# S5 mixer: a batch's output and gelu emitted one iteration later, its tables one iteration nearer; transposes tied to a matmul in the second FFN's input

## The chip, the cores and the metric

One core of one Trainium2 chip. The metric is the device time of one execution in microseconds (us). Engines: PE (TensorE, matmuls and transposes), DVE (VectorE), ACT (ScalarE), POOL (GpSimd), SP (issues DMAs).

## The reference

A decoder trunk of two layers over 512 positions of 1024 channels, float32. Layer 0 mixes by a diagonal complex state-space layer (S5), layer 1 by differential attention; each is followed by a gated convolutional FFN and a gated per-layer projection. The change lies mainly in the S5 mixer, which is:

```python
u = h @ w_in
bu_r = jnp.einsum("tbgc,gpc->tbgp", u_chunk, bb_r)
bu_i = jnp.einsum("tbgc,gpc->tbgp", u_chunk, bb_i)
pw_r, pw_i, s_r, s_i = lax.associative_scan(_ssm_combine, (a_r, a_i, bu_r, bu_i), axis=0)
x_r = s_r + pw_r * x_r0 - pw_i * x_i0
x_i = s_i + pw_r * x_i0 + pw_i * x_r0
y = einsum("tbgp,gcp->tbgc", x_r, cr) - einsum("tbgp,gcp->tbgc", x_i, ci)
...
y = y + d_skip * u
g = jax.nn.gelu(y)
val, gate = jnp.split(g @ w_glu, 2, axis=-1)
return val * jax.nn.sigmoid(gate)
```

There are 64 groups of 16 channels with 64 complex states each.

## The kernel before

All matrix products with weights are made as three float32r matmuls of a high and a low part (`mm3`, L121 to L125); ACT casts a weight tile to its high part (`hi_wst`, L107, L112), DVE makes the low part (`lo_wst`, L108, L113). A program-wide scheduler orders the instructions of each engine by the order in which they are emitted, moving one ahead of others where its operands are ready; so the order of the Python statements gives priorities, and the order that came out is shown below.

**The mixer** (`ssm`, L629 to L713) handles the 64 groups as 8 batches of 8. For batch b these steps are made, by the names that the rows carry:

- `ssm_coefs` and `cprod` (L491 to L498, DVE): the products `wo` of C and the powers. `wo` has one buffer.
- `ssm_prep` (L511 to L528): ACT spreads `wo` into zero-padded operands, `wp` (for the inputs) and `op` (for the outputs; both L504, `pad`); PE transposes `wp` (`ct`, L526, two banks), ACT copies it to `ctrl` (L527). `op` has two buffers, `wp` one.
- `ssm_tables` (L454 to L479): rotation tables `tab` of sines and cosines, DVE at L464 and L467, ACT at L466 (`rnd`) and L474 to L478 (Sin and Abs); POOL spreads the decay (L471).
- `ssm_turn_u` (L557, L559): PE transposes the batch's inputs (`ut`), ACT copies them to `uc`.
- `ssm_toep` (L530 to L550): the short-range block, PE at L536 and L546 into the bank `toep`, ACT copies at L547 and L549.
- `ssm_inputs` (L568): `v`, 16 matmuls into two banks. `ssm_states` (DVE L587, L588, L589, L591 twice, L592, L593, L596): rotate, scan, rotate back, into `xs`.
- `ssm_out` (PE L605, L609, ACT L612): `y`, then gelu into `g`. Gelu and Sin need different tables of ACT, so an ACT_TABLE_LOAD stands before the first of either kind.
- `ssm_turn` (PE L621, ACT L625, DVE L626): `g` transposed (`gt`) and split into `hTh` and `hTl` for the next product.

Steps of neighbouring batches are interleaved in one loop, b from -2 to 9. Between them PE works on two weight products in steps: the second half of `w_in` (`u1`), and the first quarter of `w_glu` (`gv`), step k of which needs `hTh`, `hTl` of batch k. The banks `ct` (both), `ut`, `toep`, `gt` and `y` all rotate over the same two PSUM banks (tag "tp"); a bank is free for the next when its reader, an ACT copy or the gelu, is done.

**The second place** is the input projection of the second FFN behind the attention (L923 to L931): `flush_turns` emits the transposes of a normed row block between the matmul steps of `project_k` (L811).

Of the kernel before, what the change touches and what calls it, by code (L numbers as in the profile page):

```python
# [10 lines left out]
F32 = mybir.dt.float32  # L11
# [7 lines left out]
P = 128  # L19
# [3 lines left out]
KD = D // P  # L23
# [33 lines left out]
class Trunk:  # L57
# [62 lines left out]
    def mm3(self, out, lhs, rhs, start, stop):  # L120
        nc = self.nc  # L121
        (ah, al), (bh, bl) = lhs, rhs
        nc.tensor.matmul(out, ah, bh, start=start, stop=False)  # L123
        nc.tensor.matmul(out, ah, bl, start=False, stop=False)  # L124
        nc.tensor.matmul(out, al, bh, start=False, stop=stop)  # L125

    def norm(self, nm):

# [382 lines left out]
    def ssm_prep(self, sp, b, coefs):  # L511

        nc = self.nc
        bc, wo = coefs
        wp = sp.tile([P, 8, 4, 2, 16], F32, tag="wp", name=f"wp{b}", bufs=1)
        self.pad(wp, wo[:, :, 0])
        op = sp.tile([P, 8, 5, 2, 16], F32, tag="op", name=f"op{b}", bufs=2)
        self.pad(op[:, :, 1:], wo[:, :, 1])
        self.pad(op[:, :, 0:1], bc[:, :, 1].rearrange("p r q (o c) -> p r q o c", o=1))
        op = op.rearrange("p (r q) n g c -> p r q (n g c)", r=2)  # L520
        wp = wp.rearrange("p (r q) n g c -> p r q (n g c)", r=2)
        ctrl = sp.tile([P, 2, 512], F32, tag="ctrl", name=f"ctrl{b}", bufs=2)
        for r in range(2):
            ps = self.bank(f"ct{b}_{r}", "tp")
            for q in range(4):
                nc.tensor.transpose(ps[:, q * P:(q + 1) * P], wp[:, r, q, :], self.ident)  # L526
            nc.scalar.copy(ctrl[:, r, :], ps)  # L527
        return ctrl, wp, op  # L528

    def ssm_toep(self, sp, b, wp, op):  # L530
# [97 lines left out]
    def ssm(self, nxt):  # L628
        nc, tc, io = self.nc, self.tc, self.io  # L629
        with ExitStack() as ctx:  # L630
            sp = ctx.enter_context(tc.tile_pool(name="ssm", bufs=1))
            st = self.ssm_load(sp)


            n, copied = Raw(self, "ssm"), []
            u0 = Accumulate(self, io["w_in"][0], "u0")
            for c in range(2):
                for j in range(4):
                    self.turn(self.x[j], j, c, "ssm", ("tp", "aux")[j % 2])
                    if c == 0:  # L640
                        copied.append(self.copied)
                for k in range(4):
                    if k % 2 == 0:
                        i = 2 * c + k // 2
                        u0.w.append(self.split(st[i], self.gssm[:, 2 * i:2 * i + 2]))
                    u0.step(4 * c + k)
                if c == 0:
                    self.ssm_params(sp)
            for j in range(4):
                with tc.issue_after(copied[j].ins):  # L650
                    n.scale(j)
            U = self.xall.rearrange("p a b -> p (a b)")
            Uv = U.rearrange("p (q j e) -> p q j e", j=4, e=32)

            def done(nb):
                def f(j, ps):
                    nc.scalar.activation(Uv[:, nb * 16:(nb + 1) * 16, 3 - j, :], ps.rearrange("p (q e) -> p q e", e=32),
                                         AF.Copy, scale=n.rs[:, j:j + 1])
                return f

            for j in range(4):
                done(0)(j, u0.ps[j])
            gv = Accumulate(self, io["w_glu"][0], "gv0")
            u1 = Accumulate(self, io["w_in"][1], "u1", g=self.gssm)

            tab, coefs, prep, toep, uc, ins, xs, gs = ({} for _ in range(8))
            on = lambda n: 0 <= n < 8
            for b in range(-2, 10):
                if on(b + 1):
                    prep[b + 1] = self.ssm_prep(sp, b + 1, coefs[b + 1])  # L670
                if on(b):
                    xs[b] = self.ssm_states(sp, b, ins[b], tab[b])
                if on(b + 1):
                    uc[b + 1] = self.ssm_turn_u(sp, b + 1, U)
                    toep[b + 1] = self.ssm_toep(sp, b + 1, *prep[b + 1][1:])
                for k in GV.get(b, ()):
                    gv.step(k)
                if on(b - 1):
                    self.ssm_turn(b - 1, gs[b - 1])
                if on(b + 1):  # L680
                    ins[b + 1] = self.ssm_inputs(b + 1, uc[b + 1], prep[b + 1][0])
                if on(b):
                    gs[b] = self.ssm_out(sp, b, prep[b][2], toep[b], uc[b], xs[b])
                if on(b + 2):
                    tab[b + 2] = self.ssm_tables(sp, b + 2)
                for k in U1.get(b, ()):
                    u1.step(k)
                    if k == KD - 1:
                        for j in range(4):
                            done(1)(j, u1.ps[j])  # L690
                if on(b + 2):
                    coefs[b + 2] = self.ssm_coefs(sp, b + 2)
            self.load_x()
            self.load_conv(0)
            for nb in range(2):
                val = {}

                def keep(t, ps):
                    if t % 2 == 0:
                        val[t // 2] = sp.tile([P, 2, 512], F32, tag="ctrl", name=f"val{nb}_{t}", bufs=2)  # L700
                    nc.scalar.copy(val[t // 2][:, t % 2], ps)

                def gate(t, ps):
                    s = sp.tile([P, 512], F32, tag="g", name=f"gate{nb}_{t}", bufs=2)
                    nc.scalar.activation(s, ps, AF.Sigmoid)
                    nc.vector.tensor_tensor(s, s, val[t // 2][:, t % 2], ALU.mult)
                    self.add_x(t, nb, s)

                if nb == 0:
                    for t in range(NT):  # L710
                        keep(t, gv.ps[t])
                else:
                    self.project(io["w_glu"][nb], f"gv{nb}", False, keep)  # L713
                self.project(io["w_glu"][nb + 2], f"gg{nb}", True, gate, nxt=nxt if nb else None, split=KD // 2 - 2 * nb,
                             behind=None if nb else self.rotated)
# [94 lines left out]

    def project_k(self, ps, w, t, k0, k1, c=slice(0, 512)):  # L811
        for k in range(k0, k1):
            self.mm3(ps[:, c], self.hT(k, t), [z[:, c] for z in self.rhs(w, k)], k == 0, k == KD - 1)

    def head_norm(self, ps, nb, t, dst, ap, nm, scale, ident, me):

# [25 lines left out]
    def attention(self, me, nxt):  # L842


        nc, tc, io = self.nc, self.tc, self.io
        with ExitStack() as ctx:
# [6 lines left out]
            c = (qT, kT, v, strip, sg, ap)  # L853
# [23 lines left out]
            for b in (keys, queries, values):  # L877
                f = b(0)
# [18 lines left out]
            wo = []  # L897
# [12 lines left out]
            n = nxt()  # L910
            w = self.weights(io["w_o"][1])
            ps = [self.bank(f"wo1_{t}") for t in range(NT)]
# [5 lines left out]
            for t in back:  # L918
                if t == 1:
                    po = self.bank("wo0_0", "aux")  # L920
                    self.project_k(po, wo, 0, 0, 4)
                    n(2)
                    self.flush_turns()  # L923
                    self.project_k(po, wo, 0, 4, KD)
                    self.add_x(0, 0, po)
                self.project_k(ps[t], w, t, 4, 6)
                if t == 1:
                    self.flush_turns()
                self.project_k(ps[t], w, t, 6, KD)
                if t in (2, 0):  # L930
                    n(t + 1)  # L931
                self.add_x(t, 1, ps[t])
# [239 lines left out]
```

## Time and profile before

| | us |
|---|---|
| median of 3 runs (1340.53 to 1341.23) | 1340.82 |
| the profiled execution | 1340.96 |
| its span in the trace | 1339.2 |
| PE busy | 1316.7 (98%) |
| DVE busy | 780.6 (58%) |
| ACT busy | 615.8 (46%) |

The profile is one execution; busy shares are means over the whole span, and the mixer, which is the first eighth of it, looks different from the rest. So the rows further down are those of the mixer's batches.

### The profile page before, as it was taken

To read this page: it belongs to the slowest core of one execution; us is meant where nothing else is said; L and a number is where in the kernel's file an instruction comes from. 1 tells how busy PE (TensorE), PEld (TensorE's weight loads), DVE (VectorE), ACT (ScalarE), POOL (GpSimd) and SP (SyncE) were. 2 spreads that over 40 slices of the span, in tenths; PEclk is the share of its full clock that TensorE was granted. 3 is DMA by queue.
4 is the path that set the end of the run, shared out by engine and by line. 5 is a ranking of instruction groups with operands and counts; after the bars stand their busy time and mean duration, and the time that the engine had idled before them with its cause. 6 is when DMAs were issued, how large, how long until landed. Compare 5 with 4: busy or idle time off the path is not lost.

```text
span 1339.2 us, 16754 instructions
## 1 busy us (share of the span) xinstructions
PE 1316.7 (98%) x6524; PEld 1084.4 (81%) x6524; DVE 780.6 (58%) x1305; ACT 615.8 (46%) x1049; POOL 90.3 (7%) x101
## 2 busy tenths in 40 slices
PE   7999899999999999999999999999999999999998
PEld 5887788987888888888887776689888888888887
DVE  8999734666633566443544665746766435664343
ACT  7899524444421444243545565635444313443241
POOL 2153000000000000000030121000000000000000
PEclk9999999999999999999999999999999999999999
DMA  6311322333333333322423102113333333333311
GB/s 220 106 41 52 111 95 79 101 94 98 92 110 94 96 99 102 100 80 94 138 85 126 63 1 86 42 47 111 111 95 95 109 95 96 98 105 95 95 56 40
DMA packets 37099, 122.31 MB, mean 91 GB/s; under 512 B 4339, under 2 KB 6387, under 8 KB 37020
## 3 DMA queue, kind: packets, MB, share of 16 engines
q1 hardware_dynamic: 35804, 119.07, 28.3%
q10 hardware_dynamic: 1184, 2.16, 0.5%
q8 instruction: 51, 0.84, 0.3%
q14 instruction: 28, 0.23, 0.1%
q0 software_dynamic: 32, 0.02, 0.0%
HBM read 119.12 MB, written 2.12 MB: 91 GB/s over the span
## 4 chain that ended last, share of the span: by engine, by line
PE 87%; DVE 9%; ACT 2%; issue 1%; DMA 0%; POOL 0%; SPq 0%; ACTq 0%; DVEq 0%
PE up L123 12%; PE up L124 12%; PE up L125 12%; PE dn L123 6%; PE dn L124 6%; PE dn L125 6%; PE pg L125 2%; PE pg L124 2%; PE pg L123 2%; PE s L982 2%; PE o L1004 1%; DVE zb L591 1%; PE k L123 1%; PE q L123 1%; PE gg L125 1%; PE gg L124 1%
## 5 line engine op out<-in xcount | busy, mean ns | idle before, releaser
L108 DVE TENSOR_TENSOR lo_wst<-wst,hi_wst 128x1024 fp32r<-128x1024 f32 x162 | 197.6, 1223 | 258.2 <-ACT hi_wst L107 257.9
L123 PE MATMUL up<-hTh,hi_wst 128*128 128x512 f32 (+1 forms) x768 | 285.6, 372 | 0.0
L124 PE MATMUL up<-hTl,hi_wst 128*128 128x512 f32 (+1 forms) x768 | 285.2, 371 | 0.0
L125 PE MATMUL up<-hTh,lo_wst 128*128 128x512 f32 (+1 forms) x768 | 285.2, 371 | 0.0
L107 ACT CAST hi_wst<-wst 128x1024 fp32r<-128x1024 f32 x162 | 169.6, 1049 | 227.7 <-PE dn L125 143.1
L123 PEld LDWEIGHTS up<-hTh,hi_wst 128*128 128x128 f32 x768 | 144.7, 188 | 25.3 <-ACT hi_wst L107 0.2
L125 PEld LDWEIGHTS up<-hTh,lo_wst 128*128 128x128 f32 x768 | 144.7, 188 | 24.9
L124 PEld LDWEIGHTS up<-hTl,hi_wst 128*128 128x128 f32 x768 | 144.7, 188 | 24.7
L123 PE MATMUL dn<-hi_wst,ih 128*128 128x512 f32 x352 | 137.6, 391 | 0.0
L124 PE MATMUL dn<-lo_wst,ih 128*128 128x512 f32 x352 | 137.0, 389 | 0.0
L125 PE MATMUL dn<-hi_wst,il 128*128 128x512 f32 x352 | 136.4, 389 | 0.0
L247 DVE SCALAR_TENSOR_TENSOR acc<-up,cw,acc 128x511 f32<-128x511 f32 x88 | 65.7, 747 | 47.8 <-ACT acc L246 47.8
L246 ACT ACTIVATE acc<-up,cw 128x512 f32<-128x512 f32 x88 | 68.5, 779 | 47.8 <-PE up L125 47.8
L254 ACT CAST ih<-acc 128x512 fp32r<-128x512 f32 x44 | 27.3, 620 | 112.9 <-DVE acc L251 112.8
L123 PEld LDWEIGHTS dn<-hi_wst,ih 128*128 128x128 f32 x352 | 66.1, 188 | 14.6 <-issue 1.0
L113 DVE SCALAR_TENSOR_TENSOR lo_wst<-wst,gains,hi_wst 128x512 fp32r<-128x512 f32 x80 | 56.1, 745 | 37.0 <-ACT hi_wst L112 37.0
L125 PEld LDWEIGHTS dn<-hi_wst,il 128*128 128x128 f32 x352 | 66.1, 188 | 13.7
L124 PEld LDWEIGHTS dn<-lo_wst,ih 128*128 128x128 f32 x352 | 66.1, 188 | 13.4
L248 DVE SCALAR_TENSOR_TENSOR acc<-up,cw,acc 128x510 f32<-128x510 f32 x88 | 65.8, 748 | 2.9
L112 ACT ACTIVATE hi_wst<-wst,gains 128x512 fp32r<-128x512 f32 x80 | 53.4, 718 | 28.0 <-PE dn L125 16.9
L250 ACT ACTIVATE acc<-acc 128x512 f32<-128x512 f32 x44 | 27.8, 632 | 64.9 <-DVE acc L248 64.8
L125 PE MATMUL pg<-hi_wst,hTl 128*128 128x512 f32 (+1 forms) x128 | 49.2, 384 | 0.0
(271 smaller groups left out, 2215.1 us busy)
## 6 DMA issues: line engine op xcount, KB each, us to landing
wst<-in_w_up SPq DMA_DIRECT2D x88, 512.0 KB, 3.6
wst<-in_w_down SPq DMA_DIRECT2D x44, 512.0 KB, 3.6
wst<-in_w_glu SPq DMA_DIRECT2D x16, 512.0 KB, 4.0
wst<-in_w_gate SPq DMA_DIRECT2D x16, 512.0 KB, 3.5
wst<-in_kv_w SPq DMA_DIRECT2D x16, 512.0 KB, 4.5
wst<-in_w_in SPq DMA_DIRECT2D x8, 512.0 KB, 6.8
wst<-in_w_q SPq DMA_DIRECT2D x8, 512.0 KB, 3.8
wst<-in_w_o SPq DMA_DIRECT2D x8, 512.0 KB, 4.4
```

The source lines that it names most:

```text
L107: nc.scalar.copy(hi, st)
L108: nc.vector.tensor_tensor(lo, st, hi.bitcast(F32), ALU.subtract)
L112: nc.scalar.activation(hi[:, c], st[:, c], AF.Copy, scale=g[:, k:k + 1])
L113: nc.vector.scalar_tensor_tensor(lo[:, c], st[:, c], g[:, k:k + 1], hi[:, c].bitcast(F32), ALU.mult, ALU.subtract)
L123: nc.tensor.matmul(out, ah, bh, start=start, stop=False)
L124: nc.tensor.matmul(out, ah, bl, start=False, stop=False)
L125: nc.tensor.matmul(out, al, bh, start=False, stop=stop)
L246: nc.scalar.activation(c, ps[s], AF.Identity, bias=self.cw[:, n, 3:4], scale=self.cw[:, n, 2:3])
L247: nc.vector.scalar_tensor_tensor(c[:, 1:], ps[s][:, :T - 1], self.cw[:, n, 1:2], c[:, 1:], ALU.mult, ALU.add)
L248: nc.vector.scalar_tensor_tensor(c[:, 2:], ps[s][:, :T - 2], self.cw[:, n, 0:1], c[:, 2:], ALU.mult, ALU.add)
L250: nc.scalar.activation(acc[0], acc[0], AF.Gelu_apprx_tanh)
L254: nc.scalar.copy(ih, acc[1])
```

## The change

Three edits:

1. In `ssm_prep` the four pads of `op` are emitted behind the transposes and the copies of `ctrl`.
2. In the loop, `ssm_tables(b+1)` stands right behind `ssm_prep(b+1)`, where before `ssm_tables(b+2)` stood near the end of iteration b; and `ssm_out` of batch b-1 stands in iteration b, behind the prep and the tables of batch b+1 and ahead of `ssm_states(b)`, where before `ssm_out(b)` stood in iteration b behind `ssm_inputs(b+1)`.
3. `project_k` returns its last matmul, and in the second FFN's input `flush_turns` at t = 1 is emitted under `tc.issue_after` of it.

```diff
--- before.py
+++ after.py
@@ -122,7 +122,7 @@
         (ah, al), (bh, bl) = lhs, rhs
         nc.tensor.matmul(out, ah, bh, start=start, stop=False)
         nc.tensor.matmul(out, ah, bl, start=False, stop=False)
-        nc.tensor.matmul(out, al, bh, start=False, stop=stop)
+        return nc.tensor.matmul(out, al, bh, start=False, stop=stop)
 
     def norm(self, nm):
 
@@ -514,10 +514,6 @@
         bc, wo = coefs
         wp = sp.tile([P, 8, 4, 2, 16], F32, tag="wp", name=f"wp{b}", bufs=1)
         self.pad(wp, wo[:, :, 0])
-        op = sp.tile([P, 8, 5, 2, 16], F32, tag="op", name=f"op{b}", bufs=2)
-        self.pad(op[:, :, 1:], wo[:, :, 1])
-        self.pad(op[:, :, 0:1], bc[:, :, 1].rearrange("p r q (o c) -> p r q o c", o=1))
-        op = op.rearrange("p (r q) n g c -> p r q (n g c)", r=2)
         wp = wp.rearrange("p (r q) n g c -> p r q (n g c)", r=2)
         ctrl = sp.tile([P, 2, 512], F32, tag="ctrl", name=f"ctrl{b}", bufs=2)
         for r in range(2):
@@ -525,6 +521,10 @@
             for q in range(4):
                 nc.tensor.transpose(ps[:, q * P:(q + 1) * P], wp[:, r, q, :], self.ident)
             nc.scalar.copy(ctrl[:, r, :], ps)
+        op = sp.tile([P, 8, 5, 2, 16], F32, tag="op", name=f"op{b}", bufs=2)
+        self.pad(op[:, :, 1:], wo[:, :, 1])
+        self.pad(op[:, :, 0:1], bc[:, :, 1].rearrange("p r q (o c) -> p r q o c", o=1))
+        op = op.rearrange("p (r q) n g c -> p r q (n g c)", r=2)
         return ctrl, wp, op
 
     def ssm_toep(self, sp, b, wp, op):
@@ -668,6 +668,9 @@
             for b in range(-2, 10):
                 if on(b + 1):
                     prep[b + 1] = self.ssm_prep(sp, b + 1, coefs[b + 1])
+                    tab[b + 1] = self.ssm_tables(sp, b + 1)
+                if on(b - 1):
+                    gs[b - 1] = self.ssm_out(sp, b - 1, prep[b - 1][2], toep[b - 1], uc[b - 1], xs[b - 1])
                 if on(b):
                     xs[b] = self.ssm_states(sp, b, ins[b], tab[b])
                 if on(b + 1):
@@ -679,10 +682,6 @@
                     self.ssm_turn(b - 1, gs[b - 1])
                 if on(b + 1):
                     ins[b + 1] = self.ssm_inputs(b + 1, uc[b + 1], prep[b + 1][0])
-                if on(b):
-                    gs[b] = self.ssm_out(sp, b, prep[b][2], toep[b], uc[b], xs[b])
-                if on(b + 2):
-                    tab[b + 2] = self.ssm_tables(sp, b + 2)
                 for k in U1.get(b, ()):
                     u1.step(k)
                     if k == KD - 1:
@@ -810,7 +809,8 @@
 
     def project_k(self, ps, w, t, k0, k1, c=slice(0, 512)):
         for k in range(k0, k1):
-            self.mm3(ps[:, c], self.hT(k, t), [z[:, c] for z in self.rhs(w, k)], k == 0, k == KD - 1)
+            mm = self.mm3(ps[:, c], self.hT(k, t), [z[:, c] for z in self.rhs(w, k)], k == 0, k == KD - 1)
+        return mm
 
     def head_norm(self, ps, nb, t, dst, ap, nm, scale, ident, me):
 
@@ -923,9 +923,10 @@
                     self.flush_turns()
                     self.project_k(po, wo, 0, 4, KD)
                     self.add_x(0, 0, po)
-                self.project_k(ps[t], w, t, 4, 6)
+                mm = self.project_k(ps[t], w, t, 4, 6)
                 if t == 1:
-                    self.flush_turns()
+                    with tc.issue_after(mm.ins):
+                        self.flush_turns()
                 self.project_k(ps[t], w, t, 6, KD)
                 if t in (2, 0):
                     n(t + 1)
```

Below, the order that came out, for the last batches. A name's first number is the batch (`ct7_1` is the second `ct` bank of batch 7), the rest tells buffers apart; `gv0_2` and its like are the weight product.

PE, the output `y5` before the change:

```order
L605 MATMUL y5_1384<-toep1_296,uc5_1197 128x128 x4
L609 MATMUL y5_1384<-op5_1160,xs5_1311 128x128 x8
L123 MATMUL gv0_0_1077<-hi_wst10_1543_1545,hTh_82 128x512
L124 MATMUL gv0_0_1077<-lo_wst10_1543_1546,hTh_82 128x512
L526 MATMUL ct7_0_1434<-ident_67,wp7_1425 128x128 x4
```

and further on in the same order, up to the first inputs `v7_0`:

```order
L526 MATMUL ct7_1_1440<-ident_67,wp7_1425 128x128 x4
L125 MATMUL gv0_2_1079<-hi_wst10_1543_1545,hTl_83 128x512
L123 MATMUL gv0_3_1080<-hi_wst10_1543_1545,hTh_82 128x512
L124 MATMUL gv0_3_1080<-lo_wst10_1543_1546,hTh_82 128x512
L125 MATMUL gv0_3_1080<-hi_wst10_1543_1545,hTl_83 128x512
L557 MATMUL ut7_1460<-ident_67,x_81 128x128 x4
L536 MATMUL toep7_1467<-op7_1428,wp7_1425 32x128 x8
L546 MATMUL toep7_1467<-dm7_1476,ident_67 32x32 x4
L621 MATMUL gt5_1498<-ident_67,g5_1397 128x128 x4
L568 MATMUL v7_0_1505<-uc7_1465,ctrl7_1433 128x128 x4
```

PE after the change, up to the same `v7_0`:

```order
L522 MATMUL ct7_0_1400<-ident_67,wp7_1396 128x128 x4
L522 MATMUL ct7_1_1406<-ident_67,wp7_1396 128x128 x4
L124 MATMUL gv0_3_1080<-lo_wst10_1543_1546,hTh_82 128x512
L125 MATMUL gv0_3_1080<-hi_wst10_1543_1545,hTl_83 128x512
L605 MATMUL y5_1431<-toep1_296,uc5_1197 128x128 x4
L609 MATMUL y5_1431<-op5_1144,xs5_1311 128x128 x8
L557 MATMUL ut7_1460<-ident_67,x_81 128x128 x4
L536 MATMUL toep7_1467<-op7_1412,wp7_1396 32x128 x8
L546 MATMUL toep7_1467<-dm7_1476,ident_67 32x32 x4
L621 MATMUL gt5_1498<-ident_67,g5_1444 128x128 x4
L568 MATMUL v7_0_1505<-uc7_1465,ctrl7_1399 128x128 x4
```

`y5` stood ahead of both `ct7`; now it stands behind both, directly ahead of `ut7` and `toep7`.

ACT before the change, from the second half of the pad `wp7` to the high part of `gt5`:

```order
L504 ACTIVATE wp7_1425<-wo7_1415,s5_87 128x32x16
L612 ACT_TABLE_LOAD
L612 ACTIVATE g5_1397<-y5_1384 128x4x4x32
L504 ACTIVATE op7_1428<-wo7_1415,s5_87 128x8x4x16 x2
L504 ACTIVATE op7_1428<-bc7_1413,s5_87 128x8x16 x2
L527 COPY ctrl7_1433<-ct7_0_1434 128x512
L527 COPY ctrl7_1433<-ct7_1_1440 128x512
L559 COPY uc7_1465<-ut7_1460 128x512
L547 COPY toep1_296<-toep7_1467 32x512
L625 CAST hTh_82<-gt5_1498 128x512
```

ACT after it, from the first copy of `ctrl7` (`wp7` and three rows of `tab7` stand just above):

```order
L523 COPY ctrl7_1399<-ct7_0_1400 128x512
L523 COPY ctrl7_1399<-ct7_1_1406 128x512
L476 ACTIVATE rnd7_1419<-ang7_1417 128x256
L477 ACTIVATE tab7_1422<-rnd7_1419,halfpi_201 128x4x64
L478 ACTIVATE tab7_1422<-rnd7_1419,halfpi_201 128x4x64
L504 ACTIVATE op7_1412<-wo7_1386,s5_87 128x8x4x16 x2
L504 ACTIVATE op7_1412<-bc7_1384,s5_87 128x8x16 x2
L612 ACT_TABLE_LOAD
L612 ACTIVATE g5_1444<-y5_1431 128x4x4x32
L559 COPY uc7_1465<-ut7_1460 128x512
L547 COPY toep1_296<-toep7_1467 32x512
L625 CAST hTh_82<-gt5_1498 128x512
```

The table load and the gelu `g5` stood ahead of `op7` and `ctrl7`; they stand behind both now. In the built program the pads `op7` wait for the last matmul of `y5` (same buffer as `op5`), `y5` waits for the first copy of `ctrl7` and `toep7` for `g5` (same PSUM bank).

DVE before the change, around the states of batch 6:

```order
L467 SCALAR_TENSOR_TENSOR ang7_1399<-rnd7_1401,ang7_1399 128x256
L493 TENSOR_TENSOR wo7_1415<-wo7_1415,wot7_1416 128x512
L496 TENSOR_TENSOR wot2_7_1420<-sp1_245,bc7_1413 128x512
L497 SCALAR_TENSOR_TENSOR wo7_1415<-wo7_1415,wot2_7_1420 128x256
L498 TENSOR_TENSOR wo7_1415<-wo7_1415,wot2_7_1420 128x256
L626 TENSOR_TENSOR hTl_83<-gt4_1367,hTh_82 128x512
L587 TENSOR_TENSOR za6_1446<-v6_0_1374,tab6_1267 128x8x127
L588 TENSOR_TENSOR zb6_1447<-v6_1_1375,tab6_1267 128x8x127
```

DVE after it:

```order
L497 SCALAR_TENSOR_TENSOR wo7_1386<-wo7_1386,wot2_7_1391 128x256
L498 TENSOR_TENSOR wo7_1386<-wo7_1386,wot2_7_1391 128x256
L467 SCALAR_TENSOR_TENSOR ang7_1417<-rnd7_1419,ang7_1417 128x256
L587 TENSOR_TENSOR za6_1446<-v6_0_1374,tab6_1285 128x8x127
L626 TENSOR_TENSOR hTl_83<-gt4_1367,hTh_82 128x512
L588 TENSOR_TENSOR zb6_1447<-v6_1_1375,tab6_1285 128x8x127
```

The low part of `gt4` (L626) stood ahead of the first state step `za6`; it stands behind it now. Behind `v7_0` on PE, and behind `hTh` of `gt5` on ACT, both orders have the same steps in the same sequence; so have all engines in the attention and the second FFN, where edit 3 stands: it moves no instruction. The instructions are the same ones in the same number, ACT's 18 table loads among them.

## Rows read from the trace of the kernel before

**Rows 1.** The page, busy time by engine: us (share of the span) x instructions.

```profile
PE 1316.7 (98%) x6524; PEld 1084.4 (81%) x6524; DVE 780.6 (58%) x1305; ACT 615.8 (46%) x1049; POOL 90.3 (7%) x101
```

**Rows 2.** Stretches: us, busy (x) of PE, PEld, DVE, ACT, POOL; clock, DMA, GB/s.

```profile
50.00:100.00 50.00, 48.60 (x348) 42.06 (x346) 50.00 (x63) 45.23 (x85) 22.12 (x16) 1.00 0.16 50
100.00:143.00 43.00, 38.13 (x281) 32.73 (x280) 42.59 (x50) 39.72 (x75) 10.78 (x17) 1.00 0.14 42
...
165.00:1339.00 1174.00, 1167.68 (x5548) 958.85 (x5546) 626.65 (x1036) 482.42 (x797) 49.34 (x46) 1.00 0.29 89
```

**Rows 3.** Timeline of DVE: start, us, engine, line, operation, count [idle before].

```profile
88.11 0.41 DVE L497 SCALAR_TENSOR_TENSOR wo<-wo,wot 128x256 f32<-128x256 f32 x1
...
105.61 1.20 DVE L588 TENSOR_TENSOR zb<-v,tab 128x1016 f32<-128x1016 f32 x1
...
128.91 0.68 DVE L491 TENSOR_TENSOR wo<-sp,bc 128x512 f32<-128x512 f32 x1
...
132.77 0.68 DVE L626 TENSOR_TENSOR hTl<-gt,hTh 128x512 fp32r<-128x512 f32 x1
...
134.50 1.20 DVE L588 TENSOR_TENSOR zb<-v,tab 128x1016 f32<-128x1016 f32 x1
...
141.67 1.23 DVE L596 TENSOR_TENSOR xs<-xs,za 128x1024 f32<-128x1024 f32 x1
145.19 0.69 DVE L626 TENSOR_TENSOR hTl<-gt,hTh 128x512 fp32r<-128x512 f32 x1 [2.29 <-ACT hTh L625]
145.80 1.20 DVE L587 TENSOR_TENSOR za<-v,tab 128x1016 f32<-128x1016 f32 x1
```

**Rows 4.** Timeline of ACT, from the pads of batch 4: columns as before.

```profile
89.93 1.32 ACT L504 ACTIVATE wp<-wo,s 128x512 f32<-128x512 f32 x2
...
92.38 1.83 ACT L657 ACTIVATE x<-u,rsx_ssm 128x512 f32<-128x512 f32 x3
...
97.07 1.09 ACT L107 CAST hi_wst<-wst 128x1024 fp32r<-128x1024 f32 x1
...
100.52 0.42 ACT L475 ACTIVATE tab<-ang 128x256 f32<-128x256 f32 x1
```

**Rows 5.** Timeline of ACT, pads of batch 7 to the toep copies.

```profile
134.69 0.71 ACT L504 ACTIVATE wp<-wo,s 128x512 f32<-128x512 f32 x1
...
136.83 1.28 ACT L612 ACT_TABLE_LOAD   x1
138.12 0.60 ACT L612 ACTIVATE g<-y 128x512 f32<-128x512 f32 x1
138.62 1.32 ACT L504 ACTIVATE op<-wo,s 128x512 f32<-128x512 f32 x2
...
140.43 1.05 ACT L527 COPY ctrl<-ct 128x512 f32<-128x512 f32 x2
...
143.97 0.57 ACT L547 COPY toep<-toep 32x512 f32<-32x512 f32 x1 [1.64 <-PE toep L546]
144.57 0.59 ACT L625 CAST hTh<-gt 128x512 fp32r<-128x512 f32 x1
145.18 1.23 ACT L549 COPY toep<-toep 32x384 f32<-32x384 f32 x3
```

**Rows 6.** Timeline of PE in batch 7.

```profile
141.64 1.94 PE L536 MATMUL toep<-op,wp 128*32 128x128 f32 x16
143.50 0.43 PE L546 MATMUL toep<-dm,ident 32*32 32x32 f32 x8
143.87 0.66 PE L621 MATMUL gt<-ident,g 128*128 128x128 f32 x4
144.36 1.95 PE L568 MATMUL v<-uc,ctrl 128*128 128x128 f32 x16
146.15 1.06 PE L605 MATMUL y<-toep,uc 128*128 128x128 f32 x8
```

**Rows 7.** Timeline of POOL, the decay copy of batch 5.

```profile
94.36 10.06 POOL L471 COPY decay<-sp 128x508 f32<-128x508 f32 x1 [6.52 <-DVE zb L591]
```

## The prediction

> **What bounds the kernel now.** I read the busy times first, then the stretches, then the timelines of the engines in the mixer. Over the whole span PE is busy 98% [rows 1], which says that time can only be lost or won where PE is idle. The stretches say where that is [rows 2]: from 165 us on PE works 1167.68 of 1174 us; in the mixer, from 50 to 143 us, it works 86.7 of 93. There DVE is the full engine: 50.00 of 50 us and 42.59 of the next 43. ACT is near behind with 45.23 of 50 and 39.72 of 43. The granted clock is 1.00 throughout, so it has no part in this. Time is therefore decided by when DVE starts the states of the last batch, L587 of batch 7: the states of batch 7 close the mixer's loop, and the steps of PE and ACT behind its `v` are the same in both orders. In the profile this start is at 145.80 us [rows 3]. Ahead of it DVE waits 2.29 us for the high part `hTh` of batch 5 on ACT, the only long wait of DVE in these batches. Whatever moves this start moves the end, because PE has no slack behind it that could take it up.
>
> **Edit 3** moves no instruction on any engine, so I cost it at nothing; nothing has to cover it.
>
> **Edits 1 and 2** add and remove no instruction either; they change who waits for whom. Before, y and gelu of batch b-1 were done while the pads and `ct` of batch b+1 were still under way. Now a single line runs through all of them: `wp` (ACT), `ct` (PE), first half of `ctrl` (ACT), `y` of two batches back (PE), `op` (ACT, its buffer is the one that y reads), table load and gelu (ACT), `toep` (PE, its bank is the one that gelu reads), `gt` (PE), `hTh` (ACT), `hTl` (DVE). Behind the waiting `op` stand on ACT the load, the gelu, `uc` and the casts; behind the waiting `toep` stand on PE `gt` and `v`, for which DVE waits. I follow this through three stretches, always to the start of L588, the second step of the states, as the low part L626 now stands ahead of that (before: ahead of L587). Durations are from start to start where rows are adjacent, so that overlaps don't count twice.
>
> *Entry, batch 4.* ACT can start `wp` of batch 4 when DVE has made L497. That started at 88.11 before [rows 3] and ended some 0.3 later; ACT started `wp` at 89.93 only, behind a load and a gelu [rows 4], which now stand behind it. In the new order DVE does 0.9 us less ahead of L497 (a state step of about 1.1, a low part of 0.61 and one short step of 0.33 leave, a weight split of about 1.1 comes in), so 87.4 is the earliest and 88.6 a late value; I take 88.0. From there to the end of `hTh` of batch 2 ACT has, one behind another: `wp` 1.2; four copies of x at 0.58, 2.3 [rows 4]; three table loads at 1.29, 3.9 [rows 5]; ten small table steps at about 0.35, 3.5 (the one shown is 0.42 alone, less when they overlap) [rows 4]; `ctrl` 1.0, two weight casts at 1.09 and `op` 1.8, in all 5.0 [rows 4, 5]; gelu 0.5, `uc` 0.5, the toep copy and `hTh` 0.6 each, 2.2 [rows 5]. That is 18.1, of which about 0.2 are overlaps; 88.0 + 17.9 = 105.9, and L626 takes 0.61 [rows 3]. So L588 of batch 4 starts at 106.5 where it started at 105.61: **+0.9** (bounds +0.3, from 87.4, and +1.5, from 88.6). That ACT starts its pads 1.9 us earlier than before is thereby used up.
>
> *Batches 5 and 6.* From L588 of batch 4 to that of batch 6 there were 28.89 us, 14.45 a batch [rows 3]. In the new order the first table step on ACT waits for DVE's L467, which now stands behind all of `wo`; `hTh` stands behind it on ACT, and L626 waits for that. The ring is: the states from L588 to the end of L596, 8.40; the step L464, 0.4; L491 up to L626, that is all of `wo` and L467, 3.86 [rows 3]; a table step 0.42 [rows 4], the toep copy 0.60 and `hTh` 0.61 [rows 5], L626 0.61 [rows 3]. Sum 14.9, with some 0.1 for the hand-overs 15.0. Twice 0.55 is **+1.1**. Nothing is lost if DVE's other steps (L492 and L587, about 1.7 together) cover the 2.2 us of ACT and L626 wholly: bound 0. Above, I let two more waits of 0.7 on ACT come in: +2.5.
>
> *The last batch.* ACT starts `wp` of batch 7 behind the toep copies, 1.23 after `hTh` of batch 4 [rows 5], while L626 takes 0.61: so 0.6 after L588 of batch 6. From the start of `wp`: 1.3 for `wp`, 0.66 for four transposes (as `gt`) and 0.5 for half of `ctrl`, with the hand-overs 2.8; `y` 2.7 (24 matmuls of a kind of which 16 take 1.79) [rows 6]; `op` 1.8, load 1.29, gelu 0.6 [rows 5]; `toep` 1.86 and 0.37, `gt` 0.66 [rows 6]; `hTh` 0.6 [rows 5]; L626 0.61 [rows 3]. Sum 13.3, with hand-overs 13.5. From L588 of batch 6 to L587 of batch 7 that makes 14.1 where there were 11.30 [rows 3]: **+2.8** (bounds +2.0, if the hand-overs cost nothing and pieces overlap by 0.6, and +4.0, if each of the ten steps hands over 0.1 later). DVE has only 8.4 us of own work in this time and waits about 5 us for `hTh` of batch 5 where it waited 2.29.
>
> *POOL and SP.* The tables take their decay copy with them: POOL makes it for batch n once L591 of batch n-2 is done, before as now, and L591 of batch n needs it some 29 us later; the longest copy took 10.06 [rows 7], so nothing. SP only changes the order of a few loads of `bc` and x, which the batch ahead covers; without that cover L491 would wait.
>
> *Sum.* 0.9 + 1.1 + 2.8 = 4.8 us. The profiled execution took 1340.96, so it would take 1345.8; the median is 0.14 lower: **1345.6**. Bounds: 0.3 + 0 + 2.0 = +2.3 and 1.5 + 2.5 + 4.0 = +8.0, so 1343.1 to 1348.8 for this case alone.
>
> **A rule on the table loads.** In the profile a load costs 1.28 and the gelu behind it starts 1.29 after it [rows 5]; both programs have 18 loads, and I price each at that. The Trainium skill (ScalarE: Activation LUTs, section "Table sets: the hidden batching unit") says that a change of the active function set costs about 2.7 us and that calls should be batched by set. By that rule, four loads on the line (three at the entry, one at the end) would add 1.4 each, an estimate of 5.6 more, some 1351; the row shows no room for it, so the trace speaks against this figure here.
>
> **The rivals.**
>
> *Parity: ACT keeps its lead.* If ACT's start 1.9 us earlier at batch 4 [rows 3, 4] is carried through batches 5 and 6 instead of being used up, the last batch's +2.8 is nearly cancelled: 4.8 - 0.9 - 1.1 - 1.9 = +0.9, 1341.7. It decides if `wp` of batch 7 starts before about 134.7, as before [rows 5]. For it: DVE, not ACT, is the full engine [rows 2], and the ring of 15.0 has pieces of DVE that may cover each other. Against it: ACT's list of 17.9 us has no gap.
>
> *Faster: the wait goes.* If `hTh` of batch 5 is there when DVE is through with batch 6, the wait of 2.29 is gone [rows 3], and with the 0.41 that DVE was idle from 100 to 143 [rows 2] the end comes 2.7 earlier: 1338.1. The point is that L596 of batch 6 ended at 142.90, so `wp` of batch 7 would have to start 13 us ahead of that, at about 130, 4.7 earlier than before. For it: gelu leaves the way of `ctrl`, and `v` could come earlier. Against it: `wp` needs DVE's `wo`, of which L491 only started at 128.91 [rows 3].
>
> *Dearer: more than the sum.* If the loads cost as by that rule, or DVE's steps are slowed beside POOL's copies, whose length goes up to 10.06 [rows 7], by 0.4 a step in ten steps: 1349.6 and up.
>
> **How the numbers follow.** A measurement of this kernel can tell about 0.2%, 2.7 us, from no change. Forecast 0.63, of which 0.03 lie below 2.7; parity 0.25; faster 0.08, of which 0.02 would still read as no change; dearer 0.04. That makes slower by over 0.2%: 0.60 + 0.04 = 0.64; within: 0.25 + 0.03 + 0.02 = 0.30; faster: 0.06. The range runs from 1340.0, which takes in the larger part of parity, to 1348.8, the upper bound of the forecast; below it lie the faster case and a little of parity, above it the dearer.
>
> **What would show it.** Right: L587 of batch 7 at about 150.6; a wait of DVE of about 5 us ahead of L626 there, named ACT `hTh`; on PE a wait of `toep` of batch 7 for gelu; the rest behind 165 us unchanged but shifted. L588 of batches 4 and 6 at 106.5 and 136.5 tell the first two terms apart. Wrong: L587 at or before 145.80, or a shift that is not there at the mixer's end and arises in the attention or the second FFN, which would mean that edit 3 does something that the order doesn't show.

## The result, and the profile after the change

The change takes 1351.72 us (median of 4 runs, 1349.98 to 1352.45) where the kernel before takes 1340.80 (4 runs, 1340.53 to 1341.23): the ratio is 1.0077, 95% interval 1.0065 to 1.0088. It is slower by some 10.9 us, where 4.8 were forecast; the direction was right, the size lies above the range. The profiled execution of the change is the fastest of its four, 1349.98 us with a span of 1348.2, 9.0 more than the span of before.

The stretches of the change, with the columns of [rows 2], the last one up to the end of the span:

```profile
50.00:100.00 50.00, 48.58 (x330) 41.39 (x329) 50.00 (x62) 44.61 (x87) 24.10 (x15) 1.00 0.17 51
100.00:143.00 43.00, 35.56 (x260) 29.96 (x259) 38.59 (x48) 38.32 (x71) 7.36 (x15) 0.96 0.10 30
143.00:165.00 22.00, 17.41 (x137) 15.71 (x137) 15.61 (x16) 8.87 (x17) 0.34 (x3) 0.92 0.15 48
165.00:1348.00 1183.00, 1176.01 (x5591) 965.83 (x5589) 631.87 (x1041) 486.17 (x803) 49.33 (x46) 1.00 0.29 91
```

Up to 100 us little differs. From 100 to 143 DVE is no longer full (38.59 of 43, before 42.59), PE has lost 2.6 us of work, and the granted clock of TensorE is 0.96, then 0.92: it was 1.00 in all of [rows 2]. Behind 165 us PE idles 7.0 us in 1183, before 6.3 in 1174.

DVE, the starts of the states and the waits of batches 4 to 7 (columns as in [rows 3]):

```profile
105.60 1.22 DVE L587 TENSOR_TENSOR za<-v,tab 128x1016 f32<-128x1016 f32 x1 [1.05 <-PE v L568]
106.74 0.68 DVE L626 TENSOR_TENSOR hTl<-gt,hTh 128x512 fp32r<-128x512 f32 x1
107.33 1.20 DVE L588 TENSOR_TENSOR zb<-v,tab 128x1016 f32<-128x1016 f32 x1
...
121.22 1.22 DVE L587 TENSOR_TENSOR za<-v,tab 128x1016 f32<-128x1016 f32 x1 [0.39 <-PE v L568]
...
137.98 1.22 DVE L587 TENSOR_TENSOR za<-v,tab 128x1016 f32<-128x1016 f32 x1 [2.35 <-PE v L568]
...
139.71 1.21 DVE L588 TENSOR_TENSOR zb<-v,tab 128x1016 f32<-128x1016 f32 x1
...
154.32 0.69 DVE L626 TENSOR_TENSOR hTl<-gt,hTh 128x512 fp32r<-128x512 f32 x1 [6.21 <-ACT hTh L625]
154.93 1.20 DVE L587 TENSOR_TENSOR za<-v,tab 128x1016 f32<-128x1016 f32 x1
156.05 1.21 DVE L588 TENSOR_TENSOR zb<-v,tab 128x1016 f32<-128x1016 f32 x1
```

L587 of batch 7 starts at 154.93, 9.1 later than before [rows 3], and within 0.1 that is the 9.0 of the span: the loss is complete when the mixer ends. By the three stretches of the forecast it is +1.7 to L588 of batch 4, +3.5 to that of batch 6 (32.38 for 28.89) and +3.9 in the last batch (15.22 for 11.30).

PE, `toep` of batches 5, 6 and 7, and `gt` behind the last:

```profile
117.40 1.93 PE L536 MATMUL toep<-op,wp 128*32 128x128 f32 x16 [3.48 <-ACT g L612]
...
132.57 3.33 PE L536 MATMUL toep<-op,wp 128*32 128x128 f32 x16 [3.47 <-ACT g L612]
...
149.24 2.96 PE L536 MATMUL toep<-op,wp 128*32 128x128 f32 x16 [3.47 <-ACT g L612]
...
152.69 0.97 PE L621 MATMUL gt<-ident,g 128*128 128x128 f32 x4
```

Each waits some 3.5 us for gelu; the forecast had named this wait for batch 7. Behind two of these waits the same 16 matmuls take 3.33 and 2.96 us instead of 1.94 [rows 6]. Stretches of 4 us around them show the granted clock there (columns as above):

```profile
128.00:132.00 4.00, 1.11 (x10) 0.87 (x9) 4.00 (x5) 3.49 (x7) 1.59 (x3) 1.00 0.01 2
132.00:136.00 4.00, 3.43 (x19) 2.60 (x20) 3.56 (x7) 3.02 (x5) 0.11 (x1) 0.61 0.00 0
...
144.00:148.00 4.00, 1.77 (x16) 1.53 (x15) 3.96 (x4) 2.70 (x6) 0.23 (x2) 1.00 0.28 75
148.00:152.00 4.00, 2.76 (x16) 2.22 (x16) 0.11 (x1) 1.65 (x3) 0.11 (x1) 0.75 0.16 60
```

PE idled most of 128 to 132; in the next 4 us the mean granted clock is 0.61, near the lower of its two levels (1.2 of 2.4 GHz). Around batch 7 it is the same with 0.75.

ACT in the last batch shows the line as a whole; only rows on the line:

```profile
138.95 1.34 ACT L504 ACTIVATE wp<-wo,s 128x512 f32<-128x512 f32 x2
...
141.75 1.07 ACT L523 COPY ctrl<-ct 128x512 f32<-128x512 f32 x2 [0.54 <-PE ct L522]
...
145.37 1.34 ACT L504 ACTIVATE op<-wo,s 128x512 f32<-128x512 f32 x2 [1.30 <-PE y L609]
...
147.30 1.28 ACT L612 ACT_TABLE_LOAD   x1
148.59 0.60 ACT L612 ACTIVATE g<-y 128x512 f32<-128x512 f32 x1
...
152.80 0.57 ACT L547 COPY toep<-toep 32x512 f32<-32x512 f32 x1 [3.13 <-PE toep L546]
153.70 0.59 ACT L625 CAST hTh<-gt 128x512 fp32r<-128x512 f32 x1 [0.33 <-PE gt L621]
```

`wp`, `ct`, `ctrl`, `y`, `op`, load, gelu, `toep`, `gt`, `hTh`: one after another, with waits of ACT at `op` and at the toep copy. From `wp` to L587 of batch 7 it is 15.98 us; 13.5 were forecast.

### The profile page after: what moved, and what is told of

Its sections match the earlier page's. It is cut to its first block, busy times and chain, and to the rows that moved or that the text cites. A ratio compares the mean times of both kernels' runs of the same rounds, so it can differ in the third digit from the quotient of the medians.

```text
span 1348.2 us, 16768 instructions
## 1 busy us (share of the span) xinstructions
PE 1318.6 (98%) x6524; PEld 1085.2 (80%) x6524; DVE 781.8 (58%) x1305; ACT 616.3 (46%) x1049; POOL 88.2 (7%) x101
## 4 chain that ended last, share of the span: by engine, by line
PE 90%; ACT 5%; DVE 3%; issue 1%; DMA 1%; SPq 0%; POOL 0%; ACTq 0%; DVEq 0%
PE up L123 12%; PE up L125 12%; PE up L124 12%; PE dn L123 6%; PE dn L125 6%; PE dn L124 6%; PE pg L124 2%; PE pg L123 2%; PE pg L125 2%; PE s L983 2%; PE o L1005 1%; PE k L123 1%; PE q L123 1%; PE gg L125 1%; PE gg L123 1%; PE gg L124 1%
## 5 line engine op out<-in xcount | busy, mean ns | idle before, releaser
L124 PEld LDWEIGHTS dn<-lo_wst,ih 128*128 128x128 f32 x352 | 66.1, 188 | 13.5
```

## The experiments

The theory (L) is this line, lengthened by the lower clock behind its waits. Rivals stand in the expectations.

**Edit 3 alone** (and `project_k` and `mm3` return the matmul):

```diff
-                self.project_k(ps[t], w, t, 4, 6)
+                mm = self.project_k(ps[t], w, t, 4, 6)
                 if t == 1:
-                    self.flush_turns()
+                    with tc.issue_after(mm.ins):
+                        self.flush_turns()
```

> Before plus edit 3 alone (the transposes tied to a matmul). The order of every engine is that of before. Theory L (one line of ct, ctrl, y, op, gelu, toep in the mixer's batches, lengthened by TensorE's lower clock behind its waits): no change, 1340.8 +- 1.5 us. Rival E (edit 3 costs time behind the mixer): 1345 to 1352 us.

1341.01 us, ratio 1.000 (0.9991 to 1.001). Edit 3 costs nothing; the rival falls.

**Edit 1 alone:** the four lines that make `op`, moved.

```diff
         self.pad(wp, wo[:, :, 0])
-        op = sp.tile([P, 8, 5, 2, 16], F32, tag="op", name=f"op{b}", bufs=2)
...
             nc.scalar.copy(ctrl[:, r, :], ps)
+        op = sp.tile([P, 8, 5, 2, 16], F32, tag="op", name=f"op{b}", bufs=2)
...
```

> Before plus edit 1 alone (op's pads behind the copies of ctrl). Theory L: y and gelu are still ahead of ct, so the line is not there; ctrl comes up to 1.8 us earlier, but toep still waits for op and v stands behind toep, so 1340.8 with -2 to +1 us, L587 of batch 7 at 144 to 147 us. Rival P (moving the pads is what delays toep): 1344 us and more.

1341.23 us, ratio 0.9999 (0.999 to 1.0008). No difference. In its profile, of a span of 1340.7, L587 of batch 7 starts at 147.34, a little behind what was expected, and DVE still waits for `hTh` of batch 5:

```profile
146.73 0.69 DVE L626 TENSOR_TENSOR hTl<-gt,hTh 128x512 fp32r<-128x512 f32 x1 [2.44 <-ACT hTh L625]
```

**Edit 1 and the tables, without the output:**

```diff
                     prep[b + 1] = self.ssm_prep(sp, b + 1, coefs[b + 1])
+                    tab[b + 1] = self.ssm_tables(sp, b + 1)
...
-                if on(b + 2):
-                    tab[b + 2] = self.ssm_tables(sp, b + 2)
```

> Before plus edit 1 and the move of the tables, with y and gelu where they were. Theory L: the waits of toep for gelu are absent, TensorE keeps its clock at 1.00, but tables behind wo cost a little in each batch and the last tables stand on ACT ahead of the toep copy: +1 to +5 us, 1342 to 1346 us. Rival T (the tables make the loss): 1349 to 1353 us.

1341.03 us, ratio 0.9998 (0.9988 to 1.0008). The tables cost nothing at all, less than either side expected.

**Edit 1 and the output, without the tables:**

```diff
+                if on(b - 1):
+                    gs[b - 1] = self.ssm_out(sp, b - 1, prep[b - 1][2], toep[b - 1], uc[b - 1], xs[b - 1])
                 if on(b):
                     xs[b] = self.ssm_states(sp, b, ins[b], tab[b])
...
-                if on(b):
-                    gs[b] = self.ssm_out(sp, b, prep[b][2], toep[b], uc[b], xs[b])
```

> Before plus edit 1 and the move of y and gelu, tables where they were. Theory L: the whole line is there, TensorE idles about 3.5 us ahead of toep in each of the last batches and its clock falls: +6 to +10 us, 1347 to 1351 us. Rival T (the tables make the loss): within 2 us of 1340.8.

1357.27 us, ratio 1.0118 (1.0103 to 1.0133): slower than the whole change. So the output's move makes the loss, and the tables' move, next to it, takes some 5.5 us off again; why it does was not followed up, and the output's move without edit 1 was not run. PE's `toep` of batches 4 to 7 and the stretch that holds three of them:

```profile
105.78 3.62 PE L536 MATMUL toep<-op,wp 128*32 128x128 f32 x16 [5.08 <-ACT g L612]
...
122.97 1.94 PE L536 MATMUL toep<-op,wp 128*32 128x128 f32 x16 [2.78 <-ACT g L612]
...
139.37 3.62 PE L536 MATMUL toep<-op,wp 128*32 128x128 f32 x16 [3.47 <-ACT g L612]
...
157.49 1.94 PE L536 MATMUL toep<-op,wp 128*32 128x128 f32 x16 [3.47 <-ACT g L612]
```

```profile
100.00:143.00 43.00, 30.39 (x206) 25.19 (x205) 34.30 (x43) 34.55 (x63) 4.57 (x12) 0.87 0.07 19
```

The expected sign and place are there, the size was put too low. Of all parts this is the only one that loses.

**The gap filled.** To price the clock by itself, PE gets useless work in the gap; the orders of PE, ACT and DVE are otherwise the change's:

```diff
-        for q in range(4):
+        for q in [0, 1, 2, 3] * (6 if b in (5, 6, 7) else 1):
             nc.tensor.transpose(ps[:, q * P:(q + 1) * P], U[:, (4 * b + q) * P:(4 * b + q + 1) * P], self.ident)
```

> The change, with the four transposes ut of batches 5 to 7 made six times over into the same bank instead of once (same result, about 2.5 us of extra TensorE work in each gap ahead of toep); the order of PE, ACT and DVE is otherwise that of the change. Theory L with the clock: TensorE is busy in most of the gap, its clock stays at 1.00, toep of batches 6 and 7 takes 1.93 instead of 3.33 and 2.96, so 2 to 4 us less than the change, 1347.5 to 1349.5 us. Rival W (only the waits cost, the clock doesn't): the time of the change, 1351.7 +- 1 us, or a little more.

1347.48 us, ratio 1.0047 (1.0035 to 1.006): 4.2 us less than the change, with more work on PE, at the lower edge of what was expected. The transposes of batch 5, `toep` of each of the batches 5 to 7, and the stretches of this run:

```profile
113.17 2.78 PE L557 MATMUL ut<-ident,x 128*128 128x128 f32 x24
117.25 1.94 PE L536 MATMUL toep<-op,wp 128*32 128x128 f32 x16 [1.30 <-ACT g L612]
...
132.44 1.93 PE L536 MATMUL toep<-op,wp 128*32 128x128 f32 x16 [1.29 <-ACT g L612]
...
148.25 1.93 PE L536 MATMUL toep<-op,wp 128*32 128x128 f32 x16 [1.29 <-ACT g L612]
```

```profile
100.00:143.00 43.00, 39.59 (x308) 34.35 (x307) 40.38 (x50) 39.00 (x73) 7.35 (x15) 1.00 0.09 30
143.00:165.00 22.00, 19.58 (x164) 18.09 (x163) 16.41 (x16) 8.81 (x17) 0.34 (x3) 1.00 0.22 72
```

`toep` still waits for gelu, now only 1.3 us behind the last transpose, but runs at full speed (the granted clock is 1.00 from 100 to 143 and from 143 to 165). The rival that only waits cost falls. Against the kernel before in the same comparison (1341.07) this run is 6.4 us slower, the change 10.9: so some 4.5 us of the 10.9 go with the lower clock, and 6.4 stay when the clock is full.

**The change once more**, unaltered, for a second profile.

> The change once more, unaltered, on the same chip: 1350 to 1352.5 us; toep of at least two of the batches 5 to 7 at more than 2.5 us, with a granted clock below 1.00 there. If the clock were 1.00 throughout, about 1347.5 us.

1352.18 us, ratio 1.0077 (1.0062 to 1.0092). This execution, of 1352.39 us, has the lower clock in batches 5 and 7 and not in 6:

```profile
117.12 3.62 PE L536 MATMUL toep<-op,wp 128*32 128x128 f32 x16 [3.49 <-ACT g L612]
...
134.70 1.93 PE L536 MATMUL toep<-op,wp 128*32 128x128 f32 x16 [3.48 <-ACT g L612]
...
150.62 3.62 PE L536 MATMUL toep<-op,wp 128*32 128x128 f32 x16 [3.48 <-ACT g L612]
...
154.74 1.11 PE L621 MATMUL gt<-ident,g 128*128 128x128 f32 x4
```

L587 of batch 7 starts at 157.23 here, 2.3 later than in the first profile, and the run is 2.4 us longer: these two executions differ by how much of the work behind the waits falls into the lower clock.

**The waits taken away, everywhere.** First the bank: `y` goes to the two banks of `v`.

```diff
-        y = self.bank(f"y{b}", "tp")
+        y = self.bank(f"y{b}", "aux")
```

> The change, with y in the two banks of v instead of those of ct, ut, toep and gt, so that toep no longer waits for gelu; op still waits for y. Theory L: toep goes beside table load and gelu, the line gets some 1.9 us shorter in each batch from the fourth on and TensorE idles about 1.6 instead of 3.5 us: 4 to 8 us less than the change, 1343 to 1348 us. Rival A (ACT's own list of work is the bound, the bank isn't): within 2 us of the change, 1350 to 1353 us.

1341.12 us, ratio 0.9999 (0.999 to 1.0008): the whole loss is gone, more than the theory expected. Then the buffer, with `dm` in another tile, so that there is room:

```diff
-        op = sp.tile([P, 8, 5, 2, 16], F32, tag="op", name=f"op{b}", bufs=2)
+        op = sp.tile([P, 8, 5, 2, 16], F32, tag="op", name=f"op{b}", bufs=3)
...
-        dm = sp.tile([32, 4, 32], F32, tag="dm", name=f"dm{b}", bufs=1)
+        dm = self.junk[:32, :256].bitcast(F32).rearrange("p (q e) -> p q e", q=4)
```

> The change, with three buffers for op instead of two (dm moves into another tile to make room), so that op does not wait for y; toep still waits for gelu. Theory L: op goes ahead of ctrl or beside y, the line loses op's 1.8 us, but not the wait for gelu: 2 to 6 us less than the change, 1346 to 1350 us. Rival B (the bank of toep alone makes the loss): within 1.5 us of the change.

1340.13 us, ratio 0.9995 (0.9985 to 1.0004): gone too, which I had not expected of this wait alone. Both together:

> Both: y in the banks of v and three buffers for op. Theory L: neither wait is left, the line is nearly that of before: within 3 us of before, 1338 to 1344 us. Rival A (ACT's list is the bound): 1347 us and more.

1341.60 us, ratio 1.0004 (0.9994 to 1.0013), no more than either. In each of the three the loss goes when a wait is taken away. What part of that is the wait itself they don't show, as the scheduler, free of one, laid another order in many batches: with three buffers it put the pads ahead of `ctrl` and steps of `gv` between `ut` and `toep`.

**The waits taken away in the last batch alone.** Here the order changes only near the end. Bank, then buffer (with `dm` as just shown):

```diff
-        y = self.bank(f"y{b}", "tp")
+        y = self.bank(f"y{b}", "aux" if b in (5,) else "tp")
```

> The change, with the output y of batch 5 alone in a bank of v, so that only toep of batch 7 is free of gelu; the order differs in the last batch alone. Theory L: entry and middle stay as in the change (L588 of batch 6 at about 139.7 us), L587 of batch 7 follows 11 to 12.5 us behind it instead of 15.2: 3 to 5 us less than the change, 1347 to 1349 us. Rival S (the full change of banks helped by the order that it gave to all batches, the wait itself is cheap): within 1.5 us of the change.

```diff
-        op = sp.tile([P, 8, 5, 2, 16], F32, tag="op", name=f"op{b}", bufs=2)
+        op = sp.tile([P, 8, 5, 2, 16], F32, tag="op" if b < 7 else "op7", name=f"op{b}", bufs=2 if b < 7 else 1)
```

> The change, with a buffer of its own for op of batch 7 alone (dm moves into another tile to make room), so that these pads don't wait for y of batch 5; toep of batch 7 still waits for gelu. Theory L: load and gelu follow y at once, 2 to 3 us earlier: L587 of batch 7 12 to 13.5 us behind L588 of batch 6, 1348 to 1350.5 us. Rival S: within 1 us of the change.

The bank for one batch: 1346.06 us, ratio 1.0035 (1.0022 to 1.0048); the buffer for one batch: 1348.49, ratio 1.0051 (1.0034 to 1.0068). L588 of batch 6, L587 and L588 of batch 7 with the other bank:

```profile
139.11 1.20 DVE L588 TENSOR_TENSOR zb<-v,tab 128x1016 f32<-128x1016 f32 x1
...
149.33 1.22 DVE L587 TENSOR_TENSOR za<-v,tab 128x1016 f32<-128x1016 f32 x1 [1.83 <-PE v L568]
...
151.06 1.21 DVE L588 TENSOR_TENSOR zb<-v,tab 128x1016 f32<-128x1016 f32 x1
```

and with the own buffer:

```profile
141.26 1.21 DVE L588 TENSOR_TENSOR zb<-v,tab 128x1016 f32<-128x1016 f32 x1
...
153.17 1.21 DVE L587 TENSOR_TENSOR za<-v,tab 128x1016 f32<-128x1016 f32 x1
154.29 1.21 DVE L588 TENSOR_TENSOR zb<-v,tab 128x1016 f32<-128x1016 f32 x1
```

From L588 of batch 6 to L587 of batch 7 it is 10.22 and 11.91 us, in the change 15.22, before 11.30. With the other bank L626 stands behind L587, not ahead of it, so the start of L588 of batch 7 compares better: 11.95 and 13.03 us, in the change 16.34. Against the change in the same comparison (1352.18) the bank takes 6.1 us off, more than the 3 to 5 expected, and the buffer 3.7, as expected; both distances to L587 are shorter than expected. `toep` of batch 7 takes 1.93 in both, so a part of each gain is the clock's.

The gain arises in the batch whose wait was taken away, which speaks for the waits; but the rival doesn't fall wholly, since the order of this batch changed as well. With the bank, half of `y5` stands ahead of `ct7`, and steps of `gv` stand between `ut7` and `toep7`; with the buffer, some of the pads `op7` stand ahead of `wp7`, and the table load for Sin stands behind `wp7`. The wait and the order that comes with it were not told apart.

**A try at a faster kernel:** three buffers for `op`, with the diff above, and `y` of batch 5 alone in a bank of `v`:

```diff
-        y = self.bank(f"y{b}", "tp")
+        y = self.bank(f"y{b}", "aux" if b == 5 else "tp")
```

> The change with three buffers for op, and y of batch 5 alone in a bank of v: meant to take the last wait of DVE for v (3.44 us with three buffers alone) down by up to 2 us. Theory L: 1338 to 1340 us, faster than before. Rival A (the toep copies and hTh of the last batch are held by ACT's own list, tables behind gelu): as with three buffers alone, 1339.5 to 1341 us, no difference from before.

1340.83 us, ratio 0.9996 (0.9987 to 1.0005): no difference from the kernel before. No kernel of this study beats it clearly.

## Why the prediction was wrong in size

*What bounds the kernel, and edit 3.* Right: the start of L587 of batch 7 and the end of the span move by the same 9 us, and edit 3 alone is at 1.000.

*The line.* Right in its members and its place. The waits of `op` for `y`, of `toep` for gelu and of DVE for `hTh` of batch 5 (6.21 us, about 5 forecast) are in the rows, the last two under the names that were given, and with either of the first two taken away in batch 7 the last stretch is 3.3 to 4.4 us shorter, though its order changes with it.

*The step that failed: "The granted clock is 1.00 throughout, so it has no part in this."* It was 1.00 in the one execution of the kernel before that was profiled, so the sum has no term for it. The line that I had drawn myself left PE without work for some 3.5 us ahead of `toep` in each of the last batches, and I priced `toep` behind it at 1.86 from a row at full clock. At the lower level it took up to 3.62, with `gt` behind it up to 1.11, on the very line that decides. The filled gap puts this at some 4.5 us of the 10.9; at full clock the time is 1347.48, inside the range. The Trainium skill (TensorE: Matmul & The Clock Gate, section "HAM oscillation — how this bites in real kernels") describes waits, there for DMA, in which TensorE's clock falls, so that the next work starts slow. The trace agrees for two of the three waits in each profile of the change, though they are waits for ACT, and it was the rule to weigh here.

*The terms, sized too low.* Without the clock's part the filled gap shows +1.6 at the entry (forecast 0.9), +1.9 in the middle (1.1) and +3.1 in the last batch (2.8), in all 6.6. These are the differences of L588 of batches 4 and 6 and L587 of batch 7 to [rows 3]. DVE and ACT in that run, with L587 of batch 5 and `hTh` of batches 2 and 3:

```profile
107.18 1.21 DVE L588 TENSOR_TENSOR zb<-v,tab 128x1016 f32<-128x1016 f32 x1
...
121.06 1.22 DVE L587 TENSOR_TENSOR za<-v,tab 128x1016 f32<-128x1016 f32 x1 [0.38 <-PE v L568]
...
137.99 1.21 DVE L588 TENSOR_TENSOR zb<-v,tab 128x1016 f32<-128x1016 f32 x1
...
152.41 1.21 DVE L587 TENSOR_TENSOR za<-v,tab 128x1016 f32<-128x1016 f32 x1
```

```profile
105.75 0.58 ACT L625 CAST hTh<-gt 128x512 fp32r<-128x512 f32 x1
...
120.95 0.59 ACT L625 CAST hTh<-gt 128x512 fp32r<-128x512 f32 x1
```

At the entry most of the difference is ACT's own list: `hTh` of batch 2 ends at 106.33, where I had 105.9. The rest is L587, which waits for `v` and holds up L626 behind it. In the middle I let the ring close through L467, `hTh` and L626, and let L587 hide beside ACT. In batch 5 that ring comes out as forecast: from 107.18 its terms put the end of `hTh` at 121.47, and it is at 121.54. But L587 starts at 121.06 only, having waited for `v`, and L626 behind it at 122.20: there the ring closes through gelu, `toep`, `gt` and `v`, the same line as in the last batch. In batch 6 both ways end together: `hTh` ends at 137.34, and L626 starts behind L587 at 137.38. So the wait of `toep` for gelu, which I had counted in the last batch alone, sets batch 5 as well. The last batch was nearly right: from the start of `wp` (138.62) to L587 it is 13.79 us at full clock, 13.5 were forecast, and 15.98 in the first profile of the change.

*The rivals.* Parity and the faster case did not come: `wp` of batch 7 started at 138.95, not before 134.7. A time in the region of the dearer case came (1349.6 and up), but not by its reasons: the loads on the line take 1.28 as before, and DVE's steps are as long as before (the longest L593 takes 1.62 in both). What the range lacked was a mechanism, a clock that answers to the waits.

*The chances.* Slower was the right side, and by the line that was named. A gain of the change was nowhere to be seen: edit 1 with the tables stands at 0.9998.

## What to carry to other kernels

Before a step is moved behind others, write down for each buffer and bank in its rotation who is next to take it: here a pad behind `y` and a `toep` behind gelu turned independent pieces into one line, and with a single further buffer, or another bank, and the order that the scheduler then laid, the loss of 10.9 us was gone. Where a new order leaves PE idle for microseconds, price the matmuls behind the gap at the lower clock too, as a bound of the sum. A profile in which the clock stands at 1.00 says so only for its own gaps, and for that one execution.

## What was not expected of the hardware

Equal waits did not bring equal clocks: of three gaps of 3.47 to 3.49 us in the same places, the first profile of the change has the lower clock behind the second and third, the second behind the first and third. What decides between them was not tried. And useless work made a kernel faster: 60 transposes more on PE, and 4.2 us less.

Nor does it take a wait as long as these. With edit 3 alone, whose order is that of before, the clock fell behind waits of 1.47 and 1.19 us (the mean from 100 to 143 is 0.96), where the profile of the kernel before shows 1.00 with waits of 1.48 and 1.19 in the same places. PE, with edit 3 alone:

```profile
124.29 1.09 PE L526 MATMUL ct<-ident,wp 128*128 128x128 f32 x8 [1.47 <-ACT wp L504]
...
126.57 1.12 PE L557 MATMUL ut<-ident,x 128*128 128x128 f32 x4 [1.19 <-ACT ctrl L527]
127.62 2.94 PE L536 MATMUL toep<-op,wp 128*32 128x128 f32 x16
```

A lower clock costs where PE is on the path: here `toep` took 2.94 us, DVE shows no wait behind it, and the span was 1338.6, no longer than before.
